# Ten norms: the reciprocal root as one power on GpSimd, and the last tile's square fed straight into its sum

## The chip, the cores and the metric

The kernel runs on one core of a Trainium2 chip. The metric is the device time of one execution in microseconds (us); lower is better. The core has five engines with a queue of instructions each: TensorE (PE in the profile, with its weight loads as PEld), VectorE (DVE), ScalarE (ACT), GpSimd (POOL), and SyncE (SP), which here issues the transfers between memory on and off the chip. An engine works through its own queue in order and waits at an instruction until what that instruction needs has been signalled.

## What is computed

Two layers of one network on 512 tokens with 1024 features, in float32. Per layer, in the reference's own words:

```python
h = rms_norm(x, norm_g[i])
(c_q, c_kv, k_rope, gate_a, z, xbc, ...) = jnp.split(h @ w_in[i], split_at, axis=-1)
o_a = mla_branch(...) * silu(gate_a)     # holds rms_norm(c_q) and rms_norm(c_kv)
o_b = ssd_branch(...)                    # ends with rms_norm(y * silu(z), ssm_norm)
o_c = dsa_branch(...) * silu(gate_c)
merged = g_a * (o_a @ w_br_a[i]) + g_b * (o_b @ w_br_b[i]) + g_c * (o_c @ w_br_c[i])
x = x + merged @ w_out[i]
x = x + sigmoid(x @ w_ple_gate[i]) * (p[i] @ w_ple[i])
```

After both layers the result is `rms_norm(x, final_norm)`. A norm is

```python
y = xf * lax.rsqrt(jnp.mean(xf * xf, axis=-1, keepdims=True) + NORM_EPS)
```

Each layer holds four norms: of its input (1024 features), of c_kv (256), of c_q (384), and of the state-space branch (1024).

## The kernel before

Activations lie as [128 features, 512 tokens], one tile of SBUF per 128 features. A product of a float32 weight tile with the activations is made of three products of parts (`mm`, L235, L236 and L243): 24 matmuls for 1024 features, each 128x512. PE's order is the order in which the code is written (`manual_schedule`); the other engines' queues are set by a scheduler, in which `high_priority` moves work up.

**A norm** has three steps. `stat_add` squares each tile on ACT (L402, L405) and adds the squares on DVE (L406) into one tile `s`. `stat_sum` sums `s` over the 128 partitions with one matmul of one column per 128 tokens (L415; each shows as two records in the trace), turns the sums into mean plus epsilon `v` on DVE (L424), and then finds 1/sqrt(v) with eleven small DVE steps on a 128x4 tile: a shift and a subtraction on the bits for a first guess (L425, L426), and three rounds of Newton's method, three steps each (L428 to L430). `stat_rows` spreads the four columns over all partitions with PE transposes (L437) into PSUM, and `normed` multiplies (L448), splits (L449 on ACT, L453 on DVE), and hands the parts to the next products.

**Around the norms** the code puts other products between the one-column matmuls and the transposes, so that PE has work while the chain runs. For c_kv in `prep` this is the second tile of c_q and the four transposes of `tokens` (L664); two further tiles that don't read the norm's result, the third of c_q and the shared keys, come after the transposes of R. The first product that reads it is that of `values`. In the same stretch of layer 0 lies `rope` for the shared key: a product with the cosines on POOL (L641), and on DVE a shuffle, a product with the sines (L643), a sum (L644) and a split (L251). The tables of cosines and sines are worked out at the start of layer 0 and come back through DRAM by transfers on SP.

**The end of layer 1** is the gate of eight tiles of x (`pgate`: 24 matmuls, then Tanh on ACT L1300, a product L1301 and a sum L1302 on DVE), followed by the final norm. The last three tiles, 5, 6 and 7 (`LAST`), are done in two halves of 256 tokens. In the second half the sum for the first half's norm stands after tile 5, its transposes after tile 6, and the first half's output (`last`: L1286 on DVE, two per transfer) is mixed into what remains. Each square is added into `s` before the sum is taken.

Of the kernel before, what the change touches and what calls it, by code (L numbers as in the profile page):

```python
"""Two layers of MLA + SSD + sparse attention with a gated merge, activations kept [feature, token]."""
# [36 lines left out]
# smallest distance that falls into each of the 32 distance buckets  # L38
# [3 lines left out]
# ---------------------------------------------------------------- columns of w_in, in the order used here  # L42
# [13 lines left out]
# units of weights: 128 partitions of up to 1024 numbers  # L56
# [13 lines left out]
for _i in range(4):  # L70
    # followed by the keys of the two heads, from w_ukv
    _unit(("uq", _i), "uq", [96 * _h + _d for _h in (2 * _i, 2 * _i + 1) for _d in range(64)])
# [15 lines left out]
# ---------------------------------------------------------------- layout of the per-feature vectors  # L88
# [8 lines left out]
def pack(i):  # L97
    """Inputs laid out for the kernel; nothing is computed."""
# [42 lines left out]
    # numbers that depend on shapes alone  # L141
# [11 lines left out]
    for k in range(5):  # L153
        c[:, 408 + k] = 4.0 * (r >= 128 - 32 * k)  # the last k groups of 32 rows
# [4 lines left out]
class Build:  # L159
# [19 lines left out]
    # ---- SBUF in slots of 2 KB per partition  # L179
# [28 lines left out]
    # ---- weights: load, split into two parts of 12 bits each whose sum is exact  # L208
# [19 lines left out]
    def mm(self, ps, w, off, acts, t=slice(0, T)):  # L228
        """ps[128 features, tokens] += W^T act over the k tiles of acts, float32 from parts"""
# [23 lines left out]
    # ---- constants and tables  # L253
    def setup(self):
# [5 lines left out]
        self.hv = c.tile([128, L * 32], F32, name="hv")  # L260
        self.ple_prep(0)
# [20 lines left out]
    def rope_tables(self):  # L282
        """cosines, and sines with their signs, 32 rows four times over; worked out as [16 frequencies x 8, 64 tokens]"""
# [16 lines left out]
        # the rounding of k may leave r a little outside of [-pi, pi]  # L300
# [17 lines left out]
    def rel_setup(self):  # L318
        """positions from the first one on, thresholds, and the steps of the distance bias from bucket to bucket"""
        nc, I, cc = self.nc, self.I, self.c  # L320
        nc.sync.dma_start(cc[:, 384:416], I["c"][:, 384:416])
        # one row per bucket and query of four
# [16 lines left out]
        # masks of 0 and 1 take the steps, masks of -1 and 1 take half of them, and half of their sum is added  # L339
# [21 lines left out]
    def rel_bias(self):  # L361
        """8 * rel_bias[bucket(pos_q - pos_k)] into DRAM as [head, query, key], by sums over the buckets'
        thresholds: 32 buckets of 4 queries are the 128 rows of a product."""
# [35 lines left out]
    # ---- root mean square over the features, for each token, on every partition (PSUM)  # L399
# [9 lines left out]
    def stat_sum(self, s, dim, cs=range(4), fill=None):  # L409
        """1 / rms, [token, block of 128 tokens]"""  # L410
# [3 lines left out]
        for c in cs:  # L414
            nc.tensor.matmul(ps[:, c:c + 1], s[:, 128 * c:128 * c + 128], self.ones[:, 0:1], start=True, stop=True)  # L415
            if fill is not None and c != cs[-1]:
                self.chunk = 2
                next(fill, None)
                self.chunk = CHUNK
        v, y, t = (self.sm([128, 4], tag=f"rs{j}") for j in range(3))  # L420
        yi = self.sm([128, 4], I32, tag="rsi")
        v, y, t, yi = (x[:, a:b] for x in (v, y, t, yi))
        with self.tc.high_priority(offset=URGENT):
            nc.vector.tensor_scalar(v, ps[:, a:b], 1.0 / dim, EPS, op0=OP.mult, op1=OP.add)  # L424
            nc.vector.tensor_scalar(yi, v.bitcast(I32), 1, None, op0=OP.logical_shift_right)  # L425
            nc.vector.tensor_scalar(y.bitcast(I32), yi, -1.0, float(0x5f3759df), op0=OP.mult, op1=OP.add)  # L426
            for _ in range(3):
                nc.vector.tensor_mul(t, y, y)  # L428
                nc.vector.scalar_tensor_tensor(t, t, -0.5, v, op0=OP.mult, op1=OP.mult)
                nc.vector.scalar_tensor_tensor(y, t, 1.5, y, op0=OP.add, op1=OP.mult)  # L430
# [9 lines left out]
    def normed(self, xs, g, R):  # L440
        """parts of x * g * R"""
# [19 lines left out]
    # ---- pieces of work are generators, which yield what they put on the tensor engine in units of 512 columns  # L461
# [14 lines left out]
    def mix(*gens):  # L476
        """in turns"""
# [8 lines left out]
    def weave(self, main, n, *tracks):  # L486
        """n pieces of main with other work, lists of (generator, cost), each spread evenly over them"""
# [14 lines left out]
    # ---- one tile of h @ w_in  # L502
# [9 lines left out]
    def gate2(self, ps):  # L512
        """2 silu"""
# [6 lines left out]
    # ---- p @ w_ple / 2 into DRAM  # L520
# [24 lines left out]
    # ---- softmax of one block of 128 queries; its transpose goes to PT  # L545
# [11 lines left out]
    def turned(self, u, qt, PT):  # L557
        """parts of the transpose of one block of 128 queries, [keys, queries]"""
# [21 lines left out]
    def attention(self, logits, V, PT, done):  # L580
        """logits(h, qt): probabilities of one block of queries; V(h, kb): [128 keys, high | low].
        Three stages, each a block of queries behind the one before; two pieces per block."""
# [31 lines left out]
    def gated(self, o, g):  # L614
        """parts of o * (g / 2)"""
# [6 lines left out]
    # ---- tiles that several branches need  # L622
    def common(self, ps):
# [7 lines left out]
        # four sets of keys, two heads of which are in use; the rotated part is common to all heads  # L631
# [5 lines left out]
    def rope(self, t, hi, lo, r=slice(0, 128)):  # L637
        """parts of the rotated rows"""
# [9 lines left out]
    def mla_rope(self, l, i):  # L648
        """the rotated part of four heads' queries"""
# [484 lines left out]
    def layer(self, l, xs, s):  # L1134
# [124 lines left out]
        for half in range(2):  # L1259
            t = slice(256 * half, 256 * half + 256)  # L1260
            cs = range(2 * half, 2 * half + 2)
            for m in range(8 - LAST, 8):
                self.pgate(l, m, x1, x1p, ws[m - 8 + LAST], t)
                self.stat_add(s, x1[m], False, t)
                if half and m == 8 - LAST:
                    y = self.stat_sum(s, 1024, range(2))
# [100 lines left out]
```

## Time and profile before

| | us |
|---|---|
| median of three timed runs | 1477.1 |
| lowest and highest of them | 1476.56, 1478.08 |
| span of the profiled execution, first to last instruction | 1478.6 |
| TensorE busy in it | 1433.6 (97%) |
| VectorE busy | 1110.5 (75%) |
| ScalarE busy | 719.6 (49%) |
| GpSimd busy | 135.5 (9%) |
| mean granted TensorE clock | 0.992 of full speed |

The profiled execution is told by its span alone; no time outside that span is shown for it. Its span is 0.1% above the median of the timed runs and 0.5 us above the highest of them. Busy shares are means over the whole span; an engine that is busy 97% of the time can still be kept waiting in a few places, and these are to be looked for one by one.

### The profile page before, as it was taken

The page shows a single profiled execution, that of the slowest core. Times are in us where ns is not written, and L with a number is a line of the kernel's source. Part 1 is how long each engine was busy: PE and PEld are TensorE (multiplying, and loading weights), DVE is VectorE, ACT ScalarE, POOL GpSimd, SP SyncE. Part 2 cuts the span into 40 slices and gives each one's busy share as a digit, 9 for nine tenths or more (in the row PEclk, how much of TensorE's full clock was granted, in tenths as well). Part 3 has the DMA queues.
Part 4 walks back from the last instruction along what each step waited for, and adds up shares of the span by engine and source line. Part 5 has one row for each costly group of instructions (what it writes and reads, how often), then busy time and mean ns, then how long its engine had stood idle before and what let it go on. Part 6 is the DMA issues. An engine that isn't in the chain of part 4 may idle for free.

```text
span 1478.6 us, 20229 instructions
## 1 busy us (share of the span) xinstructions
PE 1433.6 (97%) x7244; PEld 1154.1 (78%) x7244; DVE 1110.5 (75%) x2346; ACT 719.6 (49%) x1367; POOL 135.5 (9%) x129
## 2 busy tenths in 40 slices
PE   6899999999999999999999999999999999999996
PEld 4777877777887777888878788888788777788886
DVE  7668776997888987654475697889888898775446
ACT  7447778524665342432344476632465644342332
POOL 0000000012220221000001000000322123100000
PEclk9999999999999999999999999999999999999998
DMA  7433222443333322443353322232333333234331
GB/s 260 135 94 102 83 88 79 125 126 96 102 100 122 114 93 72 157 148 98 124 171 99 111 74 74 90 99 90 115 107 102 105 114 108 72 124 146 115 98 59
DMA packets 67610, 162.40 MB, mean 110 GB/s; under 512 B 9237, under 2 KB 21653, under 8 KB 67509
## 3 DMA queue, kind: packets, MB, share of 16 engines
q1 hardware_dynamic: 67509, 161.11, 34.8%
q8 instruction: 57, 0.93, 0.3%
q14 instruction: 44, 0.36, 0.1%
HBM read 142.27 MB, written 13.83 MB: 106 GB/s over the span
## 4 chain that ended last, share of the span: by engine, by line
PE 80%; DVE 12%; DMA 3%; ACT 3%; issue 2%; POOL 1%; SPq 0%; DVEq 0%; ACTq 0%; POOLq 0%
PE p L235 22%; PE p L243 21%; PE p L236 21%; PE p L601 3%; DVE wl L225 2%; PE p L562 2%; DVE s L1033 2%; DMA s<-cum_d 2%; DVE s L965 1%; ACT wh L224 1%; PE p L388 1%; DVE s L1036 1%; PE p L682 1%; PE p L780 1%; PE p L683 1%
## 5 line engine op out<-in xcount | busy, mean ns | idle before, releaser
L235 PE MATMUL p<-s,wh 128*128 128x512 f32 (+1 forms) x1644 | 657.3, 401 | 8.1 <-ACT wh L224 8.1
L236 PE MATMUL p<-s,wl 128*128 128x512 f32 (+1 forms) x1644 | 646.5, 394 | 1.2 <-DVE wl L225 1.2
L243 PE MATMUL p<-s,wh 128*128 128x512 f32 (+1 forms) x1644 | 432.8, 395 | 0.0
L224 ACT ACTIVATE wh<-wr 128x1024 fp32r<-128x1024 f32 (+2 forms) x214 | 223.6, 1045 | 351.6 <-PE p L243 236.2
L235 PEld LDWEIGHTS p<-s,wh 128*128 128x128 f32 x1644 | 311.3, 189 | 74.4 <-ACT wh L224 8.1
L236 PEld LDWEIGHTS p<-s,wl 128*128 128x128 f32 x1644 | 311.5, 190 | 69.2 <-DVE wl L225 2.6
L225 DVE TENSOR_TENSOR wl<-wr,wh 128x1024 fp32r<-128x1024 f32 (+2 forms) x214 | 264.1, 1234 | 119.0 <-ACT wh L224 118.1
L243 PEld LDWEIGHTS p<-s,wh 128*128 128x128 f32 x1644 | 300.4, 188 | 67.2 <-issue 2.8
L552 ACT ACTIVATE s<-s,m 128x128 f32<-128x128 f32 (+3 forms) x128 | 71.5, 558 | 66.9 <-DVE m L551 66.5
L571 ACT ACTIVATE s<-p 128x256 fp32r<-128x256 f32 (+1 forms) x192 | 65.7, 342 | 58.6 <-PE p L562 31.5
L572 DVE TENSOR_TENSOR s<-p,s 128x256 fp32r<-128x256 f32 (+1 forms) x192 | 71.6, 374 | 15.1 <-ACT s L571 13.7
L880 POOL TENSOR_TENSOR s<-s,s 128x256 f32<-128x256 f32 (+2 forms) x48 | 58.1, 1229 | 142.8 <-DMA s<-bias_d 75.2
L562 PE MATMUL p<-c,s 128*128 128x128 f32 x320 | 56.4, 274 | 5.6 <-DVE s L554 5.6
L562 PEld LDWEIGHTS p<-c,s 128*128 128x128 f32 x320 | 40.6, 140 | 23.6 <-issue 10.3
L1129 DVE SCALAR_TENSOR_TENSOR s<-s,p 128x512 f32<-128x512 f32 x48 | 32.5, 677 | 34.7 <-PE p L243 34.7
L405 ACT ACTIVATE s<-s 128x512 f32<-128x512 f32 (+1 forms) x44 | 26.2, 601 | 66.4 <-DVE s L1096 39.9
L554 DVE TENSOR_SCALAR s<-s,m 128x128 f32<-128x128 f32 (+3 forms) x128 | 52.4, 409 | 2.6
L965 DVE SCALAR_TENSOR_TENSOR s<-p,v,s 128x511 f32<-128x511 f32 (+2 forms) x72 | 53.2, 740 | 0.0
L863 DVE MATCH_REPLACE8 s<-m,s 128x256 f32<-128x256 f32 (+2 forms) x96 | 51.5, 541 | 0.0
L860 DVE MAX8 m<-s 128x8 f32<-128x256 f32 (+2 forms) x96 | 49.2, 547 | 0.0
L250 ACT ACTIVATE s<-s 128x512 fp32r<-128x512 f32 (+1 forms) x58 | 36.2, 625 | 26.1 <-DVE s L644 10.7
L251 DVE TENSOR_TENSOR s<-s,s 128x512 fp32r<-128x512 f32 (+1 forms) x58 | 43.2, 745 | 7.3 <-ACT s L250 6.9
(190 smaller groups left out, 1633.5 us busy)
## 6 DMA issues: line engine op xcount, KB each, us to landing
wr<-in_w_dram SPq DMA_DIRECT2D x204, 512.0 KB, 3.6
s<-cum_d SPq DMA_DIRECT2D x32, 256.0 KB, 3.6
s<-in_x_dram SPq DMA_DIRECT2D x16, 256.0 KB, 5.3
ple_d<-s SPq DMA_DIRECT2D x16, 256.0 KB, 3.8
s<-bias_d SPq DMA_DIRECT2D x16, 256.0 KB, 3.4
s<-ple_d SPq DMA_DIRECT2D x13, 256.0 KB, 2.7
s<-bias_d SPq DMA_DIRECT2D x16, 192.0 KB, 2.8
s<-s SPq DMA_DIRECT2D x44, 64.0 KB, 2.0
```

What stands on the lines that cost most here:

```text
L224: nc.scalar.activation(hi[:, :n], raw[:, :n], AF.Copy)
L225: nc.vector.tensor_sub(lo[:, :n], raw[:, :n], hi[:, :n].bitcast(F32))
L235: nc.tensor.matmul(ps[:, t], hi[:, c], ah[:, t], start=k == 0, stop=False)
L236: nc.tensor.matmul(ps[:, t], lo[:, c], ah[:, t], start=False, stop=False)
L243: nc.tensor.matmul(ps[:, t], hi[:, c], al[:, t], start=False, stop=k == n - 1)
L552: nc.scalar.activation(u[:, :n], u[:, :n], AF.Exp, bias=mx, scale=-1.0, accum_out=sm)
L554: nc.vector.tensor_scalar(u[:, :n], u[:, :n], rs, None, op0=OP.mult)
L562: nc.tensor.transpose(tp[:, 128 * kb:128 * kb + 128], u[:, 128 * kb:128 * kb + 128], self.ident)
L571: nc.scalar.activation(h_, src, AF.Copy)
L572: nc.vector.tensor_sub(l_, src, h_.bitcast(F32))
L880: nc.gpsimd.tensor_tensor(b[:, :n], b[:, :n], mask, OP.add)
L965: nc.vector.scalar_tensor_tensor(a[:, d:], ps[:, :T - d], w(3 - d), a[:, d:], op0=OP.mult, op1=OP.add)
```

## The change

The chain of eleven DVE steps goes. A constant tile `expo`, filled with -0.5 once at the start by POOL, takes its place as the second operand of one POOL instruction, which raises `v` to that power. DVE still makes `v`. This holds for all ten places where `stat_sum` is called.

In the two halves at the end, tile 7 is handled by a new function `tail`, at high priority. Its square isn't added into `s`; it goes into a tile of its own, `q`, and PE sums `s` and `q` into the same PSUM column with two matmuls in a row. `tail` is called right after tiles 5 and 6 of its half, so that the sums of the first half now stand before tile 5 of the second half, and its transposes after that tile.

```diff
@@ setup
+        self.expo = c.tile([128, 4], F32, name="expo")
+        nc.gpsimd.memset(self.expo[:], -0.5)
@@ stat_sum
-    def stat_sum(self, s, dim, cs=range(4), fill=None):
+    def stat_sum(self, s, dim, cs=range(4), fill=None, more=None):
...
-            nc.tensor.matmul(ps[:, c:c + 1], s[:, 128 * c:128 * c + 128], self.ones[:, 0:1], start=True, stop=True)
+            parts = [s] if more is None else [s, more]
+            for i, p in enumerate(parts):
+                nc.tensor.matmul(ps[:, c:c + 1], p[:, 128 * c:128 * c + 128], self.ones[:, 0:1], start=i == 0,
+                                 stop=p is parts[-1])
...
-            nc.vector.tensor_scalar(yi, v.bitcast(I32), 1, None, op0=OP.logical_shift_right)
-            nc.vector.tensor_scalar(y.bitcast(I32), yi, -1.0, float(0x5f3759df), op0=OP.mult, op1=OP.add)
-            for _ in range(3):
-                nc.vector.tensor_mul(t, y, y)
-                nc.vector.scalar_tensor_tensor(t, t, -0.5, v, op0=OP.mult, op1=OP.mult)
-                nc.vector.scalar_tensor_tensor(y, t, 1.5, y, op0=OP.add, op1=OP.mult)
+            nc.gpsimd.tensor_tensor(y, v, self.expo[:, a:b], OP.pow)
@@ layer, last tiles
+        def tail(half):
+            t = slice(256 * half, 256 * half + 256)
+            q = self.slot()
+            with self.tc.high_priority(offset=URGENT):
+                self.pgate(l, 7, x1, x1p, ws[LAST - 1], t)
+                nc.scalar.activation(q[:, t], x1[7][:, t], AF.Square)
+                y = self.stat_sum(s, 1024, range(2 * half, 2 * half + 2), more=q)
+            self.rel(q)
+            return y
...
-            for m in range(8 - LAST, 8):
+            for m in range(8 - LAST, 7):
                 self.pgate(l, m, x1, x1p, ws[m - 8 + LAST], t)
                 self.stat_add(s, x1[m], False, t)
                 if half and m == 8 - LAST:
-                    y = self.stat_sum(s, 1024, range(2))
-                if half and m == 9 - LAST:
                     R = self.stat_rows(y, range(2))
                     rest.extend((k, slice(0, 256), R) for k in range(0, 8, 2))
                 for _ in range(min(len(rest), 2)):
                     self.last(x1, *rest.popleft())
+            y = tail(half)
...
-        R = self.stat_rows(self.stat_sum(s, 1024, range(2, 4)), range(2, 4))
+        R = self.stat_rows(y, range(2, 4))
```

Two places show what this does to the queues. The first is the norm of c_kv in layer 0. This is DVE's queue there before, from the step that makes `v` (`m_692` from the sums in `p_674`); the steps on `s_626` and `s_627` with the sines are the shared key's rotation.

```order
L424 TENSOR_SCALAR m_692<-p_674 128x4
L643 TENSOR_TENSOR s_627<-s_627,sin 32x512
L425 TENSOR_SCALAR m_695<-m_692 128x4
L644 TENSOR_TENSOR s_626<-s_626,s_627 32x512
L426 TENSOR_SCALAR m_693<-m_695 128x4
L428 TENSOR_TENSOR m_694<-m_693 128x4
L429 SCALAR_TENSOR_TENSOR m_694<-m_694,m_692 128x4
L430 SCALAR_TENSOR_TENSOR m_693<-m_694,m_693 128x4
L428 TENSOR_TENSOR m_694<-m_693 128x4
L251 TENSOR_TENSOR s_619<-s_626,s_618 32x512
```

Of the changed kernel, DVE's queue from the same step on (its line numbers are those of the changed file: L427 makes `v`, L641 and L642 are the rotation, L446 multiplies by the norm):

```order
L427 TENSOR_SCALAR m_682<-p_664 128x4
L641 TENSOR_TENSOR s_617<-s_617,sin 32x512
L642 TENSOR_TENSOR s_616<-s_616,s_617 32x512
L251 TENSOR_TENSOR s_609<-s_616,s_608 32x512
L446 SCALAR_TENSOR_TENSOR s_721<-s_598,v,p_716 128x512
```

The step that makes `v` still stands ahead of the product with the sines, and nothing else of the norm stands behind that product until the norm is used. POOL's queue in the changed kernel from the start of the program (after its memsets) shows where the powers stand, L428, the second of them this norm's:

```order
L350 TENSOR_TENSOR s_124<-s_102 128x512
L351 TENSOR_TENSOR s_104<-s_104,s_102 128x128
L428 TENSOR_TENSOR m_317<-m_316,expo 128x4
L639 TENSOR_TENSOR s_616<-s_606,cos 32x512
L428 TENSOR_TENSOR m_683<-m_682,expo 128x4
L575 CAST s_1081<-c 128x128
```

The power follows the rotation's product with the cosines (L639 there, L641 before).

The second place is the end of layer 1 on PE. Before, the last product of tile 7 in the first half (into `p_13916`) is followed at once by tile 5 of the second half (into `p_13950`):

```order
L243 MATMUL p_13916<-s_13625,wh_13839 128x256
L235 MATMUL p_13950<-s_13358,wh_13827 128x256
L236 MATMUL p_13950<-s_13358,wl_13828 128x256
L235 MATMUL p_13950<-s_13396,wh_13827 128x256
L236 MATMUL p_13950<-s_13396,wl_13828 128x256
```

In the changed kernel the sums stand in between, two for each 128 tokens, of `s` (`s_13534`) and of tile 7's square (`s_13819`):

```order
L243 MATMUL p_13823<-s_13531,wh_13745 128x256
L419 MATMUL p_13852<-c,s_13534 128x1
L419 MATMUL p_13852<-c,s_13819 128x1
L419 MATMUL p_13852<-c,s_13534 128x1
L419 MATMUL p_13852<-c,s_13819 128x1
L235 MATMUL p_13864<-s_13264,wh_13733 128x256
L236 MATMUL p_13864<-s_13264,wl_13734 128x256
```

The sums have moved up by one tile, and PE reaches the square's sum directly behind the tile that the square is made of. Elsewhere the queues are alike but for two neighbours each: on SP one weight transfer near the end stands one place earlier, and on ACT a small Exp near the start stands behind two steps of `normed`.

## Rows read from the trace of the kernel before

**Rows 1.** The page, part 1: busy time, share of the span, instructions.

```profile
PE 1433.6 (97%) x7244; PEld 1154.1 (78%) x7244; DVE 1110.5 (75%) x2346; ACT 719.6 (49%) x1367; POOL 135.5 (9%) x129
```

**Rows 2.** Waits of PE: waiter, releaser: total us, times, longest us.

```profile
PE p L437 <- DVE m L430: 9.4, 5, 4.8
```

**Rows 3.** Timeline, layer 0's c_kv norm: start, us, what, [idle before, releaser].

```profile
59.05 0.15 DVE L424 TENSOR_SCALAR m<-p 128x4 f32<-128x4 f32 x1
...
59.25 1.28 POOL L641 TENSOR_TENSOR s<-s,cos 32x512 f32<-32x512 f32 x1 [48.02 <-DVE m L424]
...
63.10 0.60 PE L664 MATMUL p<-c,s 128*128 128x128 f32 x4
...
63.82 0.29 POOL L577 CAST s<-c 128x128 fp32r<-128x128 f32 x1 [3.29 <-PE p L664]
64.10 0.68 DVE L643 TENSOR_TENSOR s<-s,sin 32x512 f32<-32x512 f32 x1 [4.89 <-DMA sin<-rope_d]
...
68.53 0.84 PE L437 MATMUL p<-c,m 128*128 128x128 f32 x4 [4.83 <-DVE m L430]
...
72.16 0.42 PE L236 MATMUL p<-s,wl 128*128 128x512 f32 x1
```

**Rows 4.** Timeline, the same norm in layer 1.

```profile
793.15 0.15 DVE L424 TENSOR_SCALAR m<-p 128x4 f32<-128x4 f32 x1
...
797.64 0.60 PE L437 MATMUL p<-c,m 128*128 128x128 f32 x4
...
799.72 0.39 PE L236 MATMUL p<-s,wl 128*128 128x512 f32 x1
```

**Rows 5.** Windows: stretch, its length, busy by engine, granted clock, DMA share, GB/s.

```profile
69.00:72.20 3.20, 3.20 (x10) 2.52 (x9) 2.79 (x4) 1.68 (x4) 0.00 (x0) 0.50 0.34 85
...
345.50:348.90 3.40, 3.40 (x10) 2.79 (x10) 2.52 (x5) 2.13 (x3) 0.55 (x1) 0.53 0.54 190
...
556.80:560.20 3.40, 3.40 (x16) 2.73 (x15) 2.94 (x5) 1.59 (x2) 1.42 (x1) 1.00 0.50 154
```

**Rows 6.** Timeline, the input norms of layer 0 and layer 1.

```profile
30.97 0.65 PE L437 MATMUL p<-c,m 128*128 128x128 f32 x4 [0.20 <-DVE m L430]
...
762.11 0.15 DVE L424 TENSOR_SCALAR m<-p 128x4 f32<-128x4 f32 x1
...
764.59 0.62 PE L437 MATMUL p<-c,m 128*128 128x128 f32 x4 [1.58 <-DVE m L430]
```

**Rows 7.** Groups kept apart by shape: count, busy us, mean ns, idle before.

```profile
L430 DVE SCALAR_TENSOR_TENSOR m<-m,m 128x4 f32<-128x4 f32 x24 | 3.9, 162 | 0.8
...
L1080 POOL TENSOR_TENSOR s<-s,s 128x384 f32<-128x384 f32 x16 | 16.6, 1039 | 106.8 <-DVE s L1079 106.8
...
L880 POOL TENSOR_TENSOR s<-s,c 128x128 f32<-128x128 f32 x16 | 8.4, 529 | 373.1 <-DMA s<-bias_d 274.0 <-DVE wl L225 82.8 <-PE p L243 14.0
```

**Rows 8.** Timeline, the end of the program, ACT, PE and DVE.

```profile
1455.82 0.38 ACT L1300 ACTIVATE s<-p 128x256 f32<-128x256 f32 x1 [0.97 <-PE p L243]
...
1457.16 0.42 ACT L405 ACTIVATE s<-s 128x256 f32<-128x256 f32 x1 [0.95 <-DVE s L1302]
...
1458.35 0.50 PE L415 MATMUL p<-c,s 128*128 128x1 f32 x4
...
1465.20 0.38 ACT L1300 ACTIVATE s<-p 128x256 f32<-128x256 f32 x1 [0.74 <-PE p L243]
...
1468.03 0.78 PE L415 MATMUL p<-c,s 128*128 128x1 f32 x4 [2.87 <-DVE s L406]
...
1468.85 0.16 DVE L424 TENSOR_SCALAR m<-p 128x2 f32<-128x2 f32 x1 [0.96 <-PE p L415]
...
1471.32 0.66 PE L437 MATMUL p<-c,m 128*128 128x128 f32 x2 [2.51 <-DVE m L430]
```

**Rows 9.** Timeline of PE, two places inside the layers where it waited.

```profile
344.20 0.30 PE L562 MATMUL p<-c,s 128*128 128x128 f32 x1 [1.91 <-DVE s L554]
...
554.35 1.12 PE L1008 MATMUL p<-s,s 128*128 128x512 f32 x2 [1.81 <-POOL s L1052]
```

More of the change, by code (lines that the diff above doesn't have):

```diff
@@ L419, in stat_sum @@
                 self.chunk = CHUNK
-        v, y, t = (self.sm([128, 4], tag=f"rs{j}") for j in range(3))
-        yi = self.sm([128, 4], I32, tag="rsi")
-        v, y, t, yi = (x[:, a:b] for x in (v, y, t, yi))
+        v, y = (self.sm([128, 4], tag=f"rs{j}")[:, a:b] for j in range(2))
         with self.tc.high_priority(offset=URGENT):
             nc.vector.tensor_scalar(v, ps[:, a:b], 1.0 / dim, EPS, op0=OP.mult, op1=OP.add)
-            nc.vector.tensor_scalar(yi, v.bitcast(I32), 1, None, op0=OP.logical_shift_right)
-            nc.vector.tensor_scalar(y.bitcast(I32), yi, -1.0, float(0x5f3759df), op0=OP.mult, op1=OP.add)
-            for _ in range(3):
-                nc.vector.tensor_mul(t, y, y)
-                nc.vector.scalar_tensor_tensor(t, t, -0.5, v, op0=OP.mult, op1=OP.mult)
-                nc.vector.scalar_tensor_tensor(y, t, 1.5, y, op0=OP.add, op1=OP.mult)
+            nc.gpsimd.tensor_tensor(y, v, self.expo[:, a:b], OP.pow)
         return y
@@ L1260, in layer @@
             t = slice(256 * half, 256 * half + 256)
-            cs = range(2 * half, 2 * half + 2)
-            for m in range(8 - LAST, 8):
+            for m in range(8 - LAST, 7):
                 self.pgate(l, m, x1, x1p, ws[m - 8 + LAST], t)
```

## The prediction, made before the changed kernel was run

> **What bounds the kernel now.** I read the busy shares first, then PE's waits, then the timeline around each wait. PE is busy 97% of the span and VectorE 75% [rows 1], so a step taken off VectorE is worth nothing in general: it is worth something only where PE stands still for it. PE's waits name such places. Its transposes of the norm, L437, waited for the last Newton step, L430, for 9.4 us in five waits [rows 2]; there are ten norms, so at the other five PE came later than the chain did. Four of the five have rows: 4.83 us at layer 0's c_kv norm [rows 3], 0.20 and 1.58 at the two input norms [rows 6], 2.51 at the very end [rows 8]. The fifth is what is left, 0.28, at the transposes of the first half near the end.
>
> The largest wait is not the chain's length. The step that makes v (L424) was over at 59.20 [rows 3]. Next in VectorE's queue stands the product with the sines, L643, which waited until 64.10 for a transfer (idle 4.89, released by the table of sines). The eleven root steps stand behind it, mixed with the rotation's own, and PE, done with L664 since about 63.7, was held until 68.53. [...] The twin in layer 1 has no wait and shows the price: from L437 to the eighth matmul behind it 2.08 us [rows 4], in layer 0 3.63 [rows 3]. That is 1.55 us more.
>
> **The change, part by part.** *The power itself* is not in the trace. From below: a line through POOL's products of two operands, 529 ns at 128 numbers per partition and 1039 at 384 [rows 7], gives 2.0 ns a number and 0.28 us at four. [...] A gain below 0.28 is excluded, since it is one POOL instruction. I take 1.04 us, the 384-wide row, as if one power cost some 96 products: nearer to the low end, because the instruction treats four numbers and not hundreds. A handover costs 0.12 us (L664 ends at 63.70, POOL's cast that waits for it starts at 63.82 [rows 3]). The root then takes 0.12 + 1.04 + 0.12 = 1.28 us behind L424, where the eleven steps took at least 11 x 0.162 = 1.8 us [rows 7].
>
> *Layer 0's c_kv norm.* The power doesn't stand in VectorE's queue and so not behind the sines. On POOL it follows the product with the cosines, L641, which ran from 59.25 to 60.53 [rows 3]. It is done at 60.53 + 0.12 + 1.04 = 61.7, 2 us before PE is done with L664. The wait of 4.83 goes, and the half clock with it: 4.83 + 1.55 = **6.38 us**. This holds up to a power of 63.70 - 60.53 - 0.24 = 2.93 us. What is late next: the multiplication by the norm stays behind the sines on VectorE, but two tiles of products that don't need it stand on PE ahead of `values`, and their weights are older work. I expect no new wait.
>
> *The input norms.* In layer 1 L424 starts at 762.11 and the transposes at 764.59, 2.48 us later, 1.58 of them idle [rows 6]. With 0.15 for L424 the new distance is 0.15 + 1.28 = 1.43: **1.05 us**; 1.58 at most, since PE then has other work. Layer 0 gives its **0.20**; its split may come a little earlier too, for which I take nothing and up to 0.7 in the range.
>
> *The other five norms inside the layers* give nothing: the shortest PE cover with a row, layer 1's c_kv, is 797.64 - 793.15 = 4.49 us [rows 4], far over either chain. VectorE's freed time, some 18 us in all, lies beside PE's work. Nothing that PE waits for is queued behind a power on POOL; POOL is busy 9%.
>
> *The end.* Here the change both takes and gives. Before, the first half's sum stood behind a further tile, and by then the square was long there. Now PE waits behind tile 7's first half for Tanh, product, sum and square. That chain is in the trace: Tanh at 1455.82, as the tile ends, and the square over at 1457.58 [rows 8]. With a handover PE goes on at 1457.70. The first small matmul reads `s` and doesn't wait; six of the eight records come behind the square, and as four took 0.50 [rows 8] they take 0.75. So the second half starts at 1458.45, 2.63 us late. It gets back the old sum, 0.50, and the 0.28 of the fifth wait, as the power has a whole tile's time; its last tile ends 1.85 later, with Tanh at 1467.05 instead of 1465.20. Behind that the chain is shorter: the square is over 1.76 later, 1468.81, since no output steps stand between; a handover; six small records and their readout, 6/4 of 0.82 (1468.03 to 1468.85), end at 1470.16; L424's 0.16 and the root's 1.28 put the transposes at 1471.60, against 1471.32. The end **loses 0.28**. The adds of the square and the shorter root are paid back by the early stall.
>
> Whether that stall, some 1.88 us, also brings PE to half clock is open. An idle of 1.81 left it at 1.00, one of 1.91 was followed by 0.53 [rows 5, 9]. The price would be that of layer 0, 1.55. I leave it out of the forecast and put it at even chances in the range.
>
> *The rest*: one memset on an idle POOL, and neighbours exchanged on SP and ACT, cost nothing.
>
> Sum: 6.38 + 1.05 + 0.20 - 0.28 = **7.35 us**. The profiled span of 1478.6 becomes 1471.25. It is 0.1% over the median of the timed runs, so I take the same off that: 1477.1 - 7.4 = **1469.7**.
>
> **The rivals.** (A) *Slower, because a power is long.* From 2.93 us on it delays layer 0's c_kv norm; at layer 1's input and at the end each microsecond counts fully; the first half's power has one tile as cover, (9.38 - 0.78) / 3 = 2.87 us from 1455.82 to 1465.20 [rows 8], which with its readout and handovers leaves about 2.4. At 3.7 us the parts are 5.61, 0.20, -1.61, -2.94 and -1.30: zero. At 5 us they sum to -5.2, and the six covered norms begin to lose, another 0 to 5: about 1485. For it: no row shows a power, and POOL's 128-wide product takes 529 ns where a step of VectorE takes 162 [rows 7]. Against it: 3.7 us for four numbers would be 340 products' worth.
>
> (B) *The end takes the gain back.* A power of 2.4 to 3.7 us, or 2 us and a half clock behind the new stall: at 2.9 us 6.38 + 0.20 - 0.81 - 2.14 - 0.50 = 3.1, less 1.55 is 1.6: 1474 to 1475.5, around the edge of what can be told from no change.
>
> (C) *The front doesn't give.* The power stands behind L641. If that product comes to wait as long as the sines do, until 64.1, the power is done at 64.1 + 1.28 + 1.28 = 66.7 and PE still idles 3 us and keeps its half clock: the place gives 1.9, the whole 2.8, so 1474.3. Against it: L641 started at 59.25, five microseconds ahead of the sines [rows 3].
>
> (D) *A first use costs extra.* If POOL is held once before its first power, layer 0's input norm pays for what exceeds its cover; a hold as long as the 4.49 us of cover in [rows 4] would cost the root's own 1.28 us: 1471.0. The first cast of the program, 0.29 us, shows no such hold [rows 3]. [...]
>
> **How the numbers follow.** The forecast, a power of up to 2.4 us, has a chance of 0.70; A 0.11; B 0.10; C 0.05; D 0.04. The range: with a power of 0.28 the input norm gives 0.53 more, the end 0.76, the split 0.7, and if one of the old half-clock stretches [rows 5] happens to fall away, 1.55: 1466.2. On the other side stands B with half clock, 1475.5, and a little of the way to A. Low 1466.2, high 1475.8; outside lie most of A and little else. A measurement of this kernel can tell about 0.2%, 3 us, from no change. Faster by more than that is the forecast and D: 0.74. Within it are B and C: 0.15. Slower is A: 0.11.
>
> **What would show it.** Right: L437 of layer 0's c_kv norm directly behind L664 and full clock behind it; the power about 1 us; PE idle about 1.9 us behind tile 7's first half; transposes at the end within half a microsecond of their old distance from the start of that half. Wrong: powers of several microseconds with PE waiting at norms where it never did; L641 late; a new wait at `values`; half clock in the last tiles.

## The result, and the profile after

The changed kernel takes 1459.6 us (median, 1457.1 to 1460.0) where the kernel before took 1476.8 beside it: a ratio of 0.9878, 95% interval 0.9864 to 0.9892. That is 17 to 18 us faster. The forecast was 1469.7 with a range from 1466.2: the direction was right, the gain was more than twice as large as forecast, and the time lies below the range.

The page of the changed kernel, its first lines (busy time, share, instructions), against [rows 1]:

```profile
span 1458.2 us, 20141 instructions
PE 1418.0 (97%) x7252; PEld 1155.9 (79%) x7252; DVE 1092.3 (75%) x2234; ACT 719.1 (49%) x1367; POOL 145.0 (10%) x140
```

PE has eight instructions more than before and yet 15.6 us less busy time (1433.6 before). The forecast asks for a tenth of that, the 1.55 of half clock; its other terms are waits, and removing those shortens idle time, not busy time. PE's waits (line waited for: us in total, times, longest):

```profile
PE p L419 <- ACT s L1263: 3.2, 2, 1.7
...
PE p L435 <- POOL m L428: 1.4, 2, 1.0
```

The 9.4 us behind the old root [rows 2] are 1.4 behind the power (L428); a wait of 3.2 for the square (L1263) is new. Of that, 1.45 lie at the very end, where 2.87 for the adds stood before [rows 8]. Now the places that the prediction named. Layer 0's c_kv norm, timeline of all engines (start, us):

```profile
58.41 0.15 DVE L427 TENSOR_SCALAR m<-p 128x4 f32<-128x4 f32 x1
...
59.34 1.28 POOL L639 TENSOR_TENSOR s<-s,cos 32x512 f32<-32x512 f32 x1 [30.66 <-DMA cos<-rope_d]
60.70 1.01 POOL L428 TENSOR_TENSOR m<-m,expo 128x4 f32<-128x4 f32 x1
62.42 0.60 PE L662 MATMUL p<-c,s 128*128 128x128 f32 x4
62.85 0.60 PE L435 MATMUL p<-c,m 128*128 128x128 f32 x4
...
63.61 0.68 DVE L641 TENSOR_TENSOR s<-s,sin 32x512 f32<-32x512 f32 x1 [5.04 <-DMA sin<-rope_d]
...
64.89 0.39 PE L236 MATMUL p<-s,wl 128*128 128x512 f32 x1
```

The power is over at 61.71, before PE has finished the transposes L662; L435 follows without a wait, while VectorE still stands at the sines until 63.61. The first power of the program, the layer 1 input norm, and all ten powers together (min/median/max in ns):

```profile
26.82 1.86 POOL L428 TENSOR_TENSOR m<-m,expo 128x4 f32<-128x4 f32 x1 [15.96 <-DVE m L427]
```

```profile
749.71 0.15 DVE L427 TENSOR_SCALAR m<-p 128x4 f32<-128x4 f32 x1
749.95 1.01 POOL L428 TENSOR_TENSOR m<-m,expo 128x4 f32<-128x4 f32 x1 [155.66 <-DVE m L427]
751.01 0.65 PE L435 MATMUL p<-c,m 128*128 128x128 f32 x4 [0.37 <-POOL m L428]
```

```profile
L428 POOL TENSOR_TENSOR m<-m,expo x10: 695/1006/1864, 26.8 to 1450.5; 128x4 f32<-128x4 f32 x8, 128x2 f32<-128x2 f32 x2
```

The end, timeline: Tanh (L1308), the square (L1263), the sum's small matmuls (L419), the power and the transposes, of both halves:

```profile
1432.99 0.38 ACT L1308 ACTIVATE s<-p 128x256 f32<-128x256 f32 x1 [0.97 <-PE p L243]
...
1434.32 0.42 ACT L1263 ACTIVATE s<-s 128x256 f32<-128x256 f32 x1 [0.95 <-DVE s L1310]
...
1434.79 1.20 PE L419 MATMUL p<-c,s 128*128 128x1 f32 x6 [1.72 <-ACT s L1263]
...
1435.85 0.56 PE L235 MATMUL p<-s,wh 128*128 128x256 f32 x1
...
1436.27 0.69 POOL L428 TENSOR_TENSOR m<-m,expo 128x2 f32<-128x2 f32 x1 [142.59 <-DVE m L427]
...
1447.56 0.38 ACT L1308 ACTIVATE s<-p 128x256 f32<-128x256 f32 x1 [0.81 <-PE p L243]
...
1449.37 0.83 PE L419 MATMUL p<-c,s 128*128 128x1 f32 x6 [1.45 <-ACT s L1263]
...
1451.22 0.43 PE L435 MATMUL p<-c,m 128*128 128x128 f32 x2 [1.03 <-POOL m L428]
```

And stretches there (length, PE busy, instructions, granted clock):

```profile
1433.00:1435.00 2.00, 0.28 (x3) 1.00 0.03 8
1435.00:1437.00 2.00, 2.00 (x11) 0.52 0.00 0
1437.00:1439.00 2.00, 2.00 (x12) 0.50 0.00 0
1439.00:1441.00 2.00, 2.00 (x11) 0.50 0.00 0
1441.00:1443.00 2.00, 2.00 (x15) 0.77 0.00 0
```

PE idles 1.72 us for the square and then runs at a granted clock of 0.50 to 0.52 for nearly seven microseconds (0.77 is the mean of the last stretch).

**Where the 20 us of the spans went.** Take the same instruction in both traces and subtract the starts. At the readout of layer 0's c_kv sum the changed kernel is 0.64 ahead (59.05 in [rows 3], 58.41 above). At the eighth matmul behind the transposes it is 7.27 ahead (72.16 in [rows 3], 64.89 after): that norm gave 6.63. At the transposes of layer 1's input norm it is 13.58 ahead (764.59 in [rows 6], 751.01). At the Tanh of tile 7's first half it is 22.83 ahead (1455.82 in [rows 8], 1432.99), and at the last transposes 20.10 (1471.32, 1451.22): the end lost 2.73. Of the growth from 7.27 to 13.58, 1.21 is the input norm of layer 1 itself, whose wait of 1.58 [rows 6] is 0.37 above. Nothing else of the change stands on the path between those places, and yet the lead grew by another 5.1 there and by 9.25 from there to the Tanh. One part of it is a stretch at half clock that this execution doesn't have. The windows of the kernel before and after at that place:

```profile
1262.00:1268.00 6.00, 5.03 (x13) 3.49 (x14) 5.90 (x9) 1.84 (x3) 2.34 (x2) 0.72 0.29 87
```

```profile
1246.00:1252.00 6.00, 6.00 (x28) 4.90 (x27) 5.45 (x9) 2.18 (x3) 1.42 (x1) 1.00 0.29 90
```

By the starts on both sides of it that gave about 1.6. It isn't the change's doing: of the kernels below, the changed one with `pad` has a granted clock of 0.50 at this place (1246 to 1248), and the kernel before with `pad` has 1.00 (1262 to 1268). Such stretches come and go between executions. The rest comes in small steps. In the longest stretch of 128x512 products without any other work on PE, this is the first step and the last group, before and then after:

```profile
608.66 0.40 PE L236 MATMUL p<-s,wl 128*128 128x512 f32 x1
...
759.16 0.62 PE L243 MATMUL p<-s,wh 128*128 128x512 f32 x2
```

```profile
599.13 0.39 PE L236 MATMUL p<-s,wl 128*128 128x512 f32 x1
...
746.77 0.63 PE L243 MATMUL p<-s,wh 128*128 128x512 f32 x2
```

645 products lie from the one start to the other: 150.50 us before, 147.64 after, or 233.3 and 228.9 ns each, with the clock at 1.00, no wait and the same instructions in the same order. Over the whole program, taking each step from one such product's start to the next that lies between 215 and 245 ns (some 4,400), the mean is 233.34 before and 229.58 after; this mean is called the pace below. The largest form of products that read no weight tile (L562 before, L560 after) didn't change; by form (count, busy us, mean ns), before and after:

```profile
L236 PE MATMUL p<-s,wl 128*128 128x512 f32 x1596 | 635.3, 398 | 1.2 <-DVE wl L225 1.2
...
L562 PE MATMUL p<-c,s 128*128 128x128 f32 x320 | 56.4, 274 | 5.6 <-DVE s L554 5.6
```

```profile
L236 PE MATMUL p<-s,wl 128*128 128x512 f32 x1596 | 627.6, 393 | 1.2 <-DVE wl L225 1.2
...
L560 PE MATMUL p<-c,s 128*128 128x128 f32 x320 | 56.4, 274 | 6.6 <-DVE s L552 6.6
```

So the question for the experiments is why every 128x512 product came to take less time.

### The profile page after: what moved, and what is told of

Same layout as the page of the kernel before. It is cut to its first block, busy times and chain, and to the rows that moved or that the text cites. A ratio compares the mean times of both kernels' runs of the same rounds, so it can differ in the third digit from the quotient of the medians.

```text
span 1458.2 us, 20141 instructions
## 1 busy us (share of the span) xinstructions
PE 1418.0 (97%) x7252; PEld 1155.9 (79%) x7252; DVE 1092.3 (75%) x2234; ACT 719.1 (49%) x1367; POOL 145.0 (10%) x140
## 4 chain that ended last, share of the span: by engine, by line
PE 73%; DVE 17%; ACT 3%; issue 3%; DMA 2%; POOL 1%; SPq 0%; POOLq 0%; DVEq 0%; ACTq 0%
PE p L243 20%; PE p L235 19%; PE p L236 19%; DVE wl L225 3%; PE p L599 3%; PE p L560 2%; DVE s L861 2%; DVE s L1031 2%; DVE m L858 2%; DMA s<-cum_d 1%; DVE s L963 1%; ACT wh L224 1%; DVE s L1034 1%; PE p L680 1%; PE p L684 1%
## 5 line engine op out<-in xcount | busy, mean ns | idle before, releaser
L560 PE MATMUL p<-c,s 128*128 128x128 f32 x320 | 56.4, 274 | 6.6 <-DVE s L552 6.6
L560 PEld LDWEIGHTS p<-c,s 128*128 128x128 f32 x320 | 40.7, 141 | 24.0 <-issue 11.2
L251 DVE TENSOR_TENSOR s<-s,s 128x512 fp32r<-128x512 f32 (+1 forms) x58 | 42.3, 730 | 7.6 <-ACT s L250 7.3
```

Of the source, the lines that this page charges most:

```text
L560: nc.tensor.transpose(tp[:, 128 * kb:128 * kb + 128], u[:, 128 * kb:128 * kb + 128], self.ident)
```

## Experiments: the pace of the products

The built programs differ in one more thing than the diff shows. In SBUF the constants come first, then the activation slots (2 KB each), then the small statistics tiles, then the weight tiles (4 KB each). The change drops two tags of statistics tiles, 12 tiles of 32 bytes, and adds one constant. So it moves the slots up by 32 bytes and the weight tiles by 352 down.

**Absolute position.** First theory: the slots' position by 64 bytes counts. Four kernels add an unused tile of 16 bytes among the constants (it moves slots and weights) or among the statistics tiles (it moves the weights alone), with no other instruction changed.

```diff
+        pad = c.tile([128, 4], F32, name="pad")
+        nc.gpsimd.memset(pad[:], 0.0)
+        padw = self.small.tile([128, 4], F32, name="padw", tag="padw", bufs=1)
+        nc.gpsimd.memset(padw[:], 0.0)
```

The kernel before with `pad`:

> The kernel before plus one unused constant tile of 16 bytes per partition, where the change puts its exponents: everything allocated behind it, activations and weights, begins 32 bytes later and so at a multiple of 64 bytes, as in the changed kernel; the queues are the same as before's. Theory (addresses): the changed kernel's 128x512 products follow each other at a median of 229 to 230 ns where before's take 233 to 234, and PE runs ahead of before by some 12 us outside the norms and the end; if that is due to the addresses, this kernel is about 12 us faster than before, 1465, with the pace of 229 ns. Rival (less work on VectorE, or another chip or day): no change, 1477, pace 233.

The changed kernel with `pad`:

> The changed kernel plus the same unused tile, so that its activations and weights begin 32 bytes past a multiple of 64, as before's do. Addresses: the pace goes back to 233 ns and the time to about 1471, which leaves 6 us of the change itself, near the 7.4 of the prediction. Rival: it stays at 1459.6.

The kernel before with `padw`:

> The kernel before with 32 unused bytes between the activations and the weights: the weights alone move to a multiple of 64 bytes. If the weight loads set the pace: about 1465. If the streamed activations set it: 1477. If each has a part, between.

The kernel before with both:

> The kernel before with both unused tiles: the activations alone stand at a multiple of 64 bytes, the weights stay 32 past one. If the streamed activations set the pace: about 1465, 229 ns. If the weight loads set it: 1477.

Measured: ratios to before of 1.0004 (0.9992 to 1.0015), 0.9874 (0.9855 to 0.9893), 1.0020 (1.0010 to 1.0029) and 1.0018 (1.0006 to 1.0030), at a pace of 233.34, 229.55, 234.08 and 234.12 ns. The theory fell: moving everything by 32 bytes did nothing, on either kernel. But moving the weights against the slots by 32 bytes cost 0.7 ns a product. That left the distance between the two. From the first slot to the first weight tile it is 166,976 bytes before and 166,592 after: 64 and 192 more than a multiple of 256. Slots, weight tiles and the 512-byte column blocks in them are all multiples of 256 in size, so that this remainder is the same for every product.

**Distance, in both kernels.** An unused tile of n bytes between the slots and the weights:

```diff
+        gap = self.small.tile([128, n // 4], F32, name="gap", tag="gap", bufs=1)
+        nc.gpsimd.memset(gap[:], 0.0)
```

The changed kernel with 384 bytes:

> The changed kernel with 384 unused bytes per partition between the activation slots and the weight tiles, which puts back the distance between the two that the kernel before has. Nothing else differs but one memset of the unused tile. Theory LAYOUT (the distance between the moving operand and the weight tiles in SBUF sets how fast the 128x512 products follow each other, and the removed statistics tiles changed it): the products follow each other every 233.3 ns again instead of 229.6, and the time is 1469 to 1471, that is 6 to 8 under the kernel before; 11 to 12 of the changed kernel's gain are gone. Theory LESS WORK (the products run closer because VectorE issues some 90 instructions fewer): 229.6 ns and 1458.6 to 1459.6, as the changed kernel.

The kernel before with 128 bytes:

> The kernel before with 128 unused bytes per partition between the activation slots and the weight tiles, so that the distance has the same remainder by 512 bytes as in the changed kernel. LAYOUT with a pattern that repeats every 512 bytes: 229.6 ns from product to product, 1465 to 1466, 11 to 12 under the kernel before, with every wait of the kernel before still there. LAYOUT with another pattern: something else than 233.3 ns, either way. LESS WORK: 233.3 ns and 1477.

Measured: 0.9945 (0.9925 to 0.9965) at 233.33 ns, and 0.9924 (0.9905 to 0.9943) at 229.53 ns. In the long stretch, the first and then the second kernel:

```profile
601.14 0.39 PE L236 MATMUL p<-s,wl 128*128 128x512 f32 x1
...
751.64 0.63 PE L243 MATMUL p<-s,wh 128*128 128x512 f32 x2
```

```profile
608.31 0.40 PE L236 MATMUL p<-s,wl 128*128 128x512 f32 x1
...
755.95 0.62 PE L243 MATMUL p<-s,wh 128*128 128x512 f32 x2
```

150.50 us and 147.64 us: to the hundredth the times of the kernels before and after, exchanged. This settles it. VectorE's smaller load isn't the cause: the changed kernel at the old distance has the old pace, and the old kernel with all its chains has the new one. The distance was worth 11.2 us to the kernel before (0.9924 of 1478.2). What the change does apart from it is the other ratio, 0.9945: 8.1 us, with an interval of 5.2 to 11.1. The pace alone would be 4,400 x 3.8 ns = 16.7 us; a third of that doesn't reach the end: in the kernel before with 128 bytes PE is busy 15.5 less than before (1418.1 for 1433.6), but idle 50.1 us for 45.0, as it comes to its waits earlier than the other engines do (its larger waits add up to 43 us for 38).

The changed kernel at the old distance, laid on the kernel before with the same pace, also shows the change's own parts: it is 0.45 ahead at the sums of layer 0's c_kv norm and 7.00 at the eighth matmul behind the transposes, so that this norm gave 6.55; it gains 1.19 at layer 1's input norm, and loses 0.96 at the end. Two half-clock stretches of the kernel before, near 346 and 1264, are not in its execution, which gave another 2.8 by chance; 0.9 went in waits between.

**Other distances.** The kernel with the late sum (below, 1456.2 us as it is, remainder 192) with gaps of 128 and 256 bytes:

> The kernel with the late sum (the changed kernel with the first half's sum behind a tile of the second half), with 128 unused bytes between activations and weights: the distance leaves 320 by 512, which none had so far. Its own time without them is 1456.2 at 229.6 ns from product to product. If only the remainder by 128 counts (64 in it gave 233.3 three times, 96 gave 234.1 twice, 0 and thus 192 by 64 as well): 64 by 128 again, as in the changed kernel, and 229.6 ns, 1456.2. If the remainder by 256 counts: 64, as in the kernel before, 233.3 ns and 1467. If the remainder by 512 or more counts, any pace; 3 us per ns of difference from 229.6 follow in the time.

> The kernel with the late sum, with 256 unused bytes between activations and weights: the distance leaves 448 by 512, and 192 by 256 as in the changed kernel. If the remainder by 256 counts: 229.6 ns and 1456.2. If the remainder by 512 or more counts: any other pace, 3 us per ns of difference in the time, and 233.3 ns or 1467 if only 192 by 512 is good.

then with 64, 192 and 32 bytes:

> The kernel with the late sum and 64 unused bytes between activations and weights: the distance is a multiple of 256 bytes. So far the remainders 64 and 96 by 256 gave 233.3 and 234.1 ns from product to product, 192 gave 229.6. HALVES (remainders under 128 are slow, those from 128 on fast): 233 to 234 ns and 1466 to 1468. NARROW (192 alone is good): the same or worse. SMOOTH (a course with its top near 96 and its bottom near 224, 128 bytes further): about 231.5 ns, 1461 to 1462.

> The same with 192 unused bytes, remainder 128 by 256. HALVES: 229.6 ns and 1455 to 1456. NARROW: 233 to 234 ns, 1466 to 1468. SMOOTH: 233 ns, 1465 to 1467.

> The same with 32 unused bytes, remainder 224 by 256. HALVES: about 229.6 ns and 1455 to 1456. NARROW: 233 to 234 ns, 1466 to 1468. SMOOTH: 229 to 229.6 ns, 1454 to 1456, and perhaps the fastest of all.

and, as a test on a kernel without the change, the kernel before with 192 bytes:

> The kernel before, nothing of the change in it, with 192 unused bytes between activations and weights: the distance becomes a multiple of 256 bytes. LAYOUT with the remainder by 256 as what counts: 228.2 ns from product to product instead of 233.3, and 15 faster than before: 1462 to 1463, with every wait of the kernel before still there. If the remainder by 512 counts (0 here, 256 in the other kernel): another pace. If the course belongs to the changed kernel alone: 233.3 ns and 1477.

| kernel | distance by 256 bytes | pace, ns | median, us | ratio to before |
|---|---|---|---|---|
| before with 192 bytes | 0 | 228.23 | 1462.9 | 0.9894 (0.9875 to 0.9914) |
| late sum with 64 bytes | 0 | 228.22 | 1452.0 | 0.9819 (0.9804 to 0.9833) |
| late sum with 128 bytes | 64 | 233.34 | 1466.1 | 0.9918 (0.9900 to 0.9935) |
| before with 32 bytes | 96 | 234.08 | 1480.5 | 1.0020 (1.0010 to 1.0029) |
| late sum with 192 bytes | 128 | 232.51 | 1466.2 | 0.9911 (0.9896 to 0.9926) |
| late sum with 256 bytes | 192 | 229.55 | 1455.0 | 0.9842 (0.9824 to 0.9861) |
| late sum with 32 bytes | 224 | 233.02 | 1466.2 | 0.9910 (0.9894 to 0.9927) |

256 bytes more changed no pace, at remainder 64 as at 192, so the remainder by 256 is what counts among the distances tried. The three courses offered for the remainders 0, 128 and 224 all fell. Halves and narrow had 0 as slow, and it is the fastest; smooth had 224 as fast, and it is slow. What stands is the table itself and no rule. The test on the kernel before came out as expected, 1462.9 for 1462 to 1463; its remark that the remainder by 512 differs from the other kernel's was a slip, since both leave 256. The long stretch of that kernel:

```profile
606.08 0.39 PE L236 MATMUL p<-s,wl 128*128 128x512 f32 x1
...
752.31 0.62 PE L243 MATMUL p<-s,wh 128*128 128x512 f32 x2
```

146.23 us for the 645 products, 4.27 less than before, without touching a norm. Moving the weight tiles by 192 bytes gave this kernel 15.5 us, nearly twice the 8.1 of all that the change was written for.

## Experiments: the norm and the end

**Queue or length, at layer 0's c_kv norm.** The kernel before keeps its chain; three steps of the first rotation leave VectorE.

```diff
+        e, self.rot = getattr(self, "rot", nc.gpsimd), nc.vector
...
-        nc.vector.tensor_mul(b[r], b[r], self.sin[r])
-        nc.vector.tensor_add(a[r], a[r], b[r])
-        self.split(a[r], hi[r], lo[r])
+        e.tensor_tensor(b[r], b[r], self.sin[r], OP.mult)
+        e.tensor_tensor(a[r], a[r], b[r], OP.add)
+        nc.scalar.activation(hi[r], a[r], AF.Copy)
+        e.tensor_tensor(lo[r], a[r], hi[r].bitcast(F32), OP.subtract)
```

> The kernel before, whose root stays the chain of eleven VectorE steps; only the three steps of the first rotation that wait for the table of sines (product, sum, difference) run on GpSimd. So nothing stands in VectorE's queue between the readout of layer 0's c_kv sum and the chain. Theory QUEUE (PE's wait of 4.83 there came from what the chain stood behind, not from its length): the chain is over some 2.2 behind its readout, 2 before PE is ready, the wait and the half clock behind it go, and the kernel is 6.4 to 6.7 faster than before, at 1470.5 to 1471. Theory LENGTH (the eleven steps themselves hold PE, and only one short instruction in their place helps): 0 to 0.6 faster, 1476.5 to 1477.

Measured: 0.9960 (0.9945 to 0.9975), 5.9 faster (3.7 to 8.1); the spans differ by 6.3. At the eighth matmul behind the transposes it has gained 6.5, with a granted clock of 1.00 from 63 to 71; 1.3 of it go again at `values`, where PE waits 1.58 for a split on VectorE (L251), 0.21 before. The chain's last step and the transposes in its timeline:

```profile
61.10 0.17 DVE L430 SCALAR_TENSOR_TENSOR m<-m,m 128x4 f32<-128x4 f32 x1
...
63.41 0.60 PE L437 MATMUL p<-c,m 128*128 128x128 f32 x4
```

All eleven steps are over at 61.27, earlier than the power of the changed kernel (61.71). So the length of the chain cost nothing at this place; what cost was that it stood behind a product that waited for a transfer.

The other way round, the changed kernel with the old chain at this norm alone, and 128 bytes that keep the remainder at 192:

```diff
+        gap = self.small.tile([128, 32], F32, name="gap", tag="gap", bufs=1)
...
-        y = self.stat_sum(kv, 256, fill=g)
+        y = self.stat_sum(kv, 256, fill=g, chain=l == 0)
```

> The changed kernel with the old chain of VectorE steps at one norm alone, the c_kv norm of layer 0, and 128 unused bytes that make up for the tiles which the chain brings back, so that the distance between activations and weights has the same remainder by 512 bytes. By the prediction's term for this norm: 6.38 slower than the changed kernel, 1465.5 to 1466.5, with PE's wait of some 4.8 and a half clock behind it. By the two traces laid on each other: 6.7 slower. If the term is smaller and other norms gave the gain: under 4 slower. LAYOUT: 229.6 ns from product to product, as in the changed kernel.

Measured: 0.9929 (0.9908 to 0.9950) against 0.9878 for the changed kernel: 7.5 slower, at a pace of 229.58 ns; with the two intervals that is 4 to 11. The wait is back:

```profile
PE p L446 <- DVE m L439: 4.7, 1, 4.7
```

and windows behind it show PE at half clock again, up to about 73:

```profile
68.00:70.00 2.00, 2.00 (x6) 1.55 (x6) 1.86 (x3) 1.08 (x3) 0.00 (x0) 0.50 0.30 75
70.00:72.00 2.00, 2.00 (x6) 1.58 (x5) 2.00 (x5) 1.66 (x5) 0.00 (x0) 0.50 0.48 152
```

Laid on the changed kernel's trace, 7.4 are lost at these products: 4.7 of wait, and 2.6 of half clock where the kernel before paid 1.55.

**The end.** The changed kernel with the end of the kernel before (tile 7 not taken ahead, its square added to the running sum, the first half's sum behind a further tile):

```diff
-            for m in range(8 - LAST, 7):
+            for m in range(8 - LAST, 8):
...
-            y = tail(half)
+                    y = self.stat_sum(s, 1024, range(2))
```

> The changed kernel with the end of the layer as the kernel before has it: the powers stay, tile 7's square goes into the running sum again and the first half's sum stands behind a further tile. It tells what the edit of the end costs. By the traces (start of tile 7's first half to the end: 22.56 before, 20.25 of it regained or lost as the two are laid on each other) the edit of the end costs 2.3: this kernel is at about 1457.3, 2.3 under the changed kernel, and PE doesn't fall to half clock near 1436. By the prediction's own term for the end, a loss of 0.28 with the shorter root in it, this kernel gives 0.3 to 1 less than the changed kernel at most: 1459 to 1460.

And with the square still apart, but the first half's sum behind the next tile (the first half's output then follows in one piece behind the transposes, not two parts per tile):

```diff
-                y = self.stat_sum(s, 1024, range(2 * half, 2 * half + 2), more=q)
-            self.rel(q)
-            return y
+            return q
...
+                if half and m == 8 - LAST:
+                    y = self.stat_sum(s, 1024, range(2), more=q)
+                if half and m == 9 - LAST:
                     R = self.stat_rows(y, range(2))
...
+                    for k in range(0, 8, 2):
+                        self.last(x1, k, slice(0, 256), R)
```

> The changed kernel, with one thing moved: the first half's sum (with its square apart, as in the changed kernel) stands behind the first tile of the second half, and its row steps behind the next one. So PE doesn't stand idle behind tile 7's first half. If the stall of some 1.9 there and the half clock behind it are what the end costs, both go: 3 to 4 under the changed kernel, 1455.5 to 1456.5, and no stretch at half clock in the last tiles. If the prediction's balance is right (the stall is paid back later by the shorter chain at the very end), the early stall alone goes: 1457.5 to 1458. If neither: 1459.6.

Measured: 0.9848 (0.9829 to 0.9867) and 0.9843 (0.9826 to 0.9860), against 0.9878 (0.9864 to 0.9892) of the changed kernel: by the ratios 4.4 and 5.2 faster than it. The second one's interval just clears that of the changed kernel, the first one's doesn't quite. The gaps of the section before bear the second out: with 256 bytes, the same remainder, it is 0.9842 again, and with 128 bytes, at the old remainder, 0.9918, where the changed kernel at the old distance is 0.9945. Neither has the early wait nor half clock where the changed kernel has both; of the second, PE's two remaining waits at the end, and a window there:

```profile
1446.07 1.44 PE L419 MATMUL p<-c,s 128*128 128x1 f32 x6 [1.64 <-ACT s L1262]
...
1448.54 0.69 PE L435 MATMUL p<-c,m 128*128 128x128 f32 x2 [1.03 <-POOL m L428]
```

```profile
1435.00:1437.00 2.00, 2.00 (x19) 1.00 0.00 0
1437.00:1439.00 2.00, 2.00 (x20) 1.00 0.00 0
```

So the edit of the end costs time, and its loss is the early stall with the half clock behind it. The two differ from each other by less than the runs can tell; no gain of feeding the square around the sum is shown.

How long that half clock lasts is not fixed. The changed kernel at the old distance has the same wait of 1.72, and behind it these windows, and the second half's first product and last Tanh:

```profile
1447.00:1449.00 2.00, 1.79 (x14) 0.89 0.00 0
1449.00:1451.00 2.00, 2.00 (x11) 0.50 0.00 0
1451.00:1453.00 2.00, 2.00 (x15) 0.76 0.00 0
```

```profile
1447.90 0.36 PE L235 MATMUL p<-s,wh 128*128 128x256 f32 x1
...
1458.21 0.38 ACT L1310 ACTIVATE s<-p 128x256 f32<-128x256 f32 x1 [0.70 <-PE p L243]
```

That is some three and a half microseconds at the low level, and 10.31 us from the one to the other, against nearly seven and 11.71 (1435.85 to 1447.56) in the changed kernel.

With 64 bytes of gap the late sum is the fastest kernel of this study, 1452.0 us at 0.9819 (0.9804 to 0.9833), faster than both kernels of the case.

## Why the prediction was wrong, and where it was right

**The step that failed is the sum itself, in "the rest ... cost nothing".** It costed instructions, queues and waits, and took the duration of every untouched product as given. The change drops 384 bytes of statistics tiles, the weight tiles move against the slots, and every 128x512 product follows the one before 3.8 ns sooner. That term is about 10 us: 9.9 by the ratios 0.9945 and 0.9878, with their intervals 6 to 13.5, and 10.7 between the spans of the changed kernel at the old distance (1468.9) and as it is (1458.2). With the distance held, a gain of 7.35 was forecast and 8.1 (5.2 to 11.1) was measured. The parts fit too, the end with some luck: in the trace at the old distance the two norms gave 6.55 and 1.19 for 6.38 and 1.05, and the end lost 0.96 for 0.28, as a half clock that the sum left out and a shorter last chain than worked out partly cancel. So the direction came from a part that was understood, and the error from one that was not looked at.

**The power** was taken as 1.04 us and took 1.01 at the norms with a row of four, 0.69 with two. The low end of 0.28 and rivals A and B, which needed 2 us and more, are out. (B's times were narrower than its condition: by the prediction's own sums a power of 2.4 us alone leaves a gain of 4.6, 1472.5, and one of 3.7 leaves none, 1477.1.) Rival D is out too: the first power started 0.16 us behind the end of the step that makes `v` and took 1.86, 0.86 more than the usual one, and PE didn't wait for it.

**Layer 0's c_kv norm**, forecast 6.38: the traces give 6.63, the chain put back alone costs 7.5, and the experiment on the queue gives 5.9. The mechanism is shown from both sides: not the chain's length, but its place behind the sines, and half clock behind the wait. The 1.55 for that half clock is what one trace showed, where 0.50 was granted from 69.00 to 72.20 [rows 5], behind an idle of 4.83; with the chain put back it lasted to 73 and cost 2.6. The end of the power, forecast 61.7, was 61.71. Rival C is out: L639 started at 59.34.

**The input norms**, forecast 1.05 and 0.20: in layer 1 the idle of 1.58 [rows 6] is 0.37, so 1.21; layer 0 gave its small part within the 0.64 that the start of the program gained.

**The end** was mis-sized: a loss of 0.28 was forecast, 2.73 is what the starts give, and 0.96 at the old distance. The early stall came out as worked out, 1.72 for 1.88. The chain at the very end was even shorter than forecast, 3.66 from the Tanh to the transposes where 4.55 was worked out. The half clock was left out at even chances and came in both kernels; its price was taken from layer 0 as 1.55. Between the first half's small matmuls and the second half's Tanh 11.71 us passed (1435.85 to 1447.56), against 8.60 worked out: 3.1 of price, twice the term, since the low clock lasted nearly seven microseconds here. At the old distance it lasted half as long, and the 10.31 leave 1.7, close to the term. So the term was the price of a short stretch, and none of the prediction's rows showed a longer one.

**What the range missed**: it allowed for one old half-clock stretch to fall away (one did in this execution, near 1264, about 1.6, though not by the change), but it had no case in which PE's own work gets faster.

## What to carry to other kernels

A change that adds or drops even a small tile can move the buffers that are laid out behind it, as here the weight tiles by 352 bytes, so compare not only waits but the pace of untouched products in both traces: divide a long stretch of equal products by their number. To learn what an edit itself does, give the layout back with an unused tile of the same size; and where a kernel is bound by matmuls that stream from SBUF, try a few gaps of 32 to 192 bytes between activations and weights before tuning instructions (192 bytes gave the kernel before 15.5 us here). In an in-order queue look at what the short chain stands behind before counting its steps (here a wait of 4.89 us for a transfer [rows 3]), and price a stall as a range: behind the same wait of 1.72 us the low clock cost 1.7 in one execution and 3.1 in another.

## What the runs showed of the hardware

The pace of a 128x512 product, the mean of the steps of 215 to 245 ns, went from 228.2 to 234.1 ns with nothing but the distance between its two operands in SBUF. By its remainder of 256 bytes, 0 (228.2) and 192 (229.5 to 229.6) were fast, 64 (233.3), 96 (234.1), 128 (232.5) and 224 (233.0) slow; the same 645 products took 150.50 us at 64 and 146.23 at 0. Absolute position didn't count where both moved by 32 bytes: 233.34 ns with and without `pad` in the kernel before, 229.55 and 229.58 in the changed one. The cause inside the chip is open: the records of the weight loads themselves last 188 to 190 ns on average before and after, and no run here took the loads apart from the products. A distance that is a multiple of 512 wasn't tried.

In the changed kernel a power of 128x4 on GpSimd took 1.01 us and one of 128x2 0.69, with 1.86 for the first in the program.
